# A two-layer hybrid backbone on one core: w_out, the first quarter and the last quarter of the MLP issued in two parts of the tokens

## The chip, the cores and the metric

The kernel runs on one core of one Trainium2 chip. The metric is the device time of one execution in microseconds (us). A profile of one execution comes with it. The engines are TensorE (PE, with its weight loads as PEld), VectorE (DVE), ScalarE (ACT), GpSimd (POOL) and SyncE (SP), which only issues transfers here.

## The reference, cut to what matters

There are 512 latent tokens and 256 context tokens of 1024 channels, and two layers. In layer 0 all 768 tokens are carried through; in layer 1 only the 512 latent ones are (the context is still projected where keys and values need it). A layer is a mixer and an MLP, each with a norm ahead of it and a norm behind it:

```python
hl = modulate(xl, norm_mix_pre[l], mod_l[0], mod_l[1])
oc, ol = token_mixer(hc, hl, cos, sin, w_in[l], rw, cv, at, w_branch[l], w_out[l], ctx_out)
xl = xl + mod_l[2] * rms_norm(ol, norm_mix_post[l])
hl = modulate(xl, norm_mlp_pre[l], mod_l[3], mod_l[4])
xl = xl + mod_l[5] * rms_norm(sq_relu_mlp(hl, w_ff1[l], w_ff2[l]), norm_mlp_post[l])
```

The mixer ends with `jnp.sum(gates * proj, axis=-2) @ w_out`, the MLP is `jnp.square(jax.nn.relu(h @ w1)) @ w2` with 4096 hidden channels. `rms_norm` needs the mean square over all 1024 channels of a token, so it can't begin for a token before the last block of output channels of that token is there. All is float32.

## The kernel before, in words

**Layout.** Activations lie with channels on the partitions and tokens along the free axis: a tensor of 1024 channels is 8 tiles (KT) of 128 x 768. Tokens 0 to 255 are the context, 256 to 767 the latents; `T` is 768 (TOK) in layer 0 and 512 (SEQ) in layer 1.

**A product** of a 128-column block of weights with all tokens is `gemm` (L378) or a `job` (L392) that `fill` (L397) issues one k-step at a time. Weights and activations are split into a high and a low fp32r part, and each of the 8 k-steps issues three products (high x high, high x low, low x high) for each piece of tokens. `pieces` (L117) gives two pieces of 384 tokens in layer 0 and one of 512 in layer 1; a piece lies in one bank of PSUM. So a block is 48 matmuls of 384 columns in layer 0 and 24 of 512 in layer 1.

**Weights** come in halves of 512 x 128 (256 KB), two to a block. `weight_half` (L369) loads one into `raw` (SP queue, L372), ACT rounds it to `wh` (L328) and DVE subtracts to make `wl` (L332). `raw` has two buffers (`nraw`), `wh` and `wl` have three each (`nw`, both set at L1081). Each product that is issued loads its own weights, also the one that is issued again for another piece or another part of the tokens.

**The stages around the change.** `merge_phase` (L1237) multiplies the three branches by w_branch into `acc`, halves `acc` (L1318), splits it, and issues w_out (jobs, L1326); `done` (L1322) copies each block back to `acc`, and `ss_slow` (L313) sums the squares (adds on POOL, a product with ones at L311 for the last two blocks). `rstd` (L281) makes the reciprocal root of the row: a row copy on ACT, small matmuls that turn the row into columns (L291), 12 short DVE instructions, and transposes that spread the result over the partitions (L298). `mlp_phase` (L1335) then loads the residual X, scales and adds it (`post_norm`, L352; L359 and L361), sums squares again, and norms (`norm_h`, L334) into `hh` and `hl`. Only then can w_ff1 begin. The MLP runs in four quarters of the hidden channels: 8 blocks of w_ff1 (L1357) and 8 blocks of w_ff2 (L1371), the latter accumulating into `acc`. After the last quarter the same tail follows: `rstd`, `post_norm`, and in layer 0 the next layer's `norm_h` (L1391), in layer 1 transposes and the store (`store_x`, L1407).

Modulation vectors of layer 0 are made by 16 steps (`mod_steps`, L220) spread over branch 1 and w_out; those of layer 1 by 24 steps over the first three quarters of layer 0's MLP.

**Order.** The program is written in one order, and the tile framework orders it again when it compiles: each engine's queue is fixed then, by a cost model and by priority, the priority being the program's order. On the chip each engine runs its queue in order. In layer 1's mixer `weave` (L1047) issues k-steps of the projection between the steps of the scan, by a ratio; `spills` (L1155) hand it the blocks of q, k, v and of the gates.

Of the kernel before, what the change touches and what calls it, by code (L numbers as in the profile page):

```python
# [18 lines left out]
D = 1024  # L19
# [57 lines left out]
class Kern:  # L77
# [255 lines left out]

    def norm_h(s, sp, X, R, T, gs, sh, hh, hl):  # L334

        nc = s.nc
        o = TOK - T
        for k in range(KT):
            t = sp.tile([128, TOK], F32, tag="nt", name="nt", bufs=2)
            for b, t0, t1 in s.pieces(T, CTX):  # L340
                v = 1 if t0 < CTX else 0
                sl = slice(t0, t1)
                nc.vector.scalar_tensor_tensor(out=t[:, sl], in0=X[:, k, sl], scalar=gs[:, k, v:v + 1], in1=R[:, b, :t1 - t0], op0=ALU.mult, op1=ALU.mult)
                if k % 2:
                    nc.scalar.activation(out=t[:, sl], in_=t[:, sl], func=AF.Identity, bias=sh[:, k, v:v + 1])
                else:
                    nc.scalar.activation(out=hh[:, k, sl], in_=t[:, sl], func=AF.Identity, bias=sh[:, k, v:v + 1])  # L347
                    nc.vector.scalar_tensor_tensor(out=hl[:, k, sl], in0=t[:, sl], scalar=sh[:, k, v:v + 1], in1=hh[:, k, sl].bitcast(F32), op0=ALU.add, op1=ALU.subtract)
            if k % 2:
                s.split(hh[:, k, o:], hl[:, k, o:], t[:, o:], True)  # L350

    def post_norm(s, sp, A, X, R, T, gm, each):  # L352

        nc = s.nc
        o = TOK - T
        for k in range(KT):
            for b, t0, t1 in s.pieces(T, CTX):
                v = 1 if t0 < CTX else 0
                nc.vector.scalar_tensor_tensor(out=A[:, k, t0:t1], in0=A[:, k, t0:t1], scalar=gm[:, k, v:v + 1], in1=R[:, b, :t1 - t0], op0=ALU.mult, op1=ALU.mult)  # L359
            eng = nc.gpsimd if k % 2 else nc.vector  # L360
            eng.tensor_tensor(out=X[:, k, o:], in0=X[:, k, o:], in1=A[:, k, o:], op=ALU.add)  # L361
            each(k)
# [29 lines left out]
    def job(s, src, mh, ml, T, done, pre=None):  # L392

        s.halves += [(src, h) for h in range(2)]
        s.jobs += [(k, mh, ml, T, done, pre) for k in range(KT)]

    def fill(s, n=1):  # L397
        nc = s.nc
        for _ in range(min(n, len(s.jobs))):
            k, mh, ml, T, done, pre = s.jobs.pop(0)  # L400
            if k % 4 == 0:
                while s.halves and len(s.ready) < s.nw:
                    s.ready.append(s.weight_half(*s.halves.pop(0)))
                s.cur = s.ready.pop(0)
            if k == 0:
                s.jps = s.mm()
                s.jctx = (pre(),) if pre else ()
            wh, wl = s.cur
            for w, m, f in ((wh, mh, 0), (wh, ml, 1), (wl, mh, 2)):
                a = m(k)  # L410
                for b, t0, t1 in s.pieces(T):
# [651 lines left out]
    def spill(s, l, r, T):  # L1063

        c0, t, f = s.spills[r]
        T = TOK if t else T
        s.in_job(l, c0, T, lambda ps: s.spill_done(r, T, f, ps))

    def spill_done(s, r, T, tanh, ps):
        nc = s.nc  # L1070
        ft = s.stage()
        if tanh:
            nc.scalar.activation(out=s.dv(ft, T), in_=s.pv(ps, T), func=AF.Tanh, scale=0.5)
        else:
            nc.scalar.activation(out=s.dv(ft, T), in_=s.pv(ps, T), func=AF.Copy)
        nc.scalar.dma_start(s.z[128 * r:128 * r + 128, TOK - T:], ft[:, TOK - T:])


    def run(s):
# [13 lines left out]
        s.z = s.dp.tile([128 * len(s.spills), TOK], F32, name="z")  # L1093
        s.kp = lambda d: d.rearrange("(k p) t -> p k t", p=128)
# [15 lines left out]
        for l in range(DEPTH):  # L1110
# [5 lines left out]
            s.h_open()  # L1116
            s.mlp_phase(l, PP, T, acc, actx)
# [9 lines left out]
    def rwkv_phase(s, l, P, T):  # L1127
# [3 lines left out]
        with ExitStack() as rc:  # L1131
# [21 lines left out]
            todo = list(range(20)) + list(range(28, 36)) + list(range(20, 28))  # L1153

            def spills(n):  # L1155
                for r in todo[:n]:
                    s.spill(l, r, T)
# [79 lines left out]
    def merge_phase(s, l, PP, T, acc):  # L1237
# [4 lines left out]
        with ExitStack() as mc:  # L1242
# [67 lines left out]
            drive(ln, 3)  # L1310
            s.fill(len(s.jobs))
            branch(1, *operand(lambda k: cvx[k]))
            for j in range(KT):
                s.fill(8)
                if steps:
                    steps.pop(0)()
            for k in range(KT):
                nc.vector.tensor_scalar(out=acc[:, k, o:], in0=acc[:, k, o:], scalar1=0.5, scalar2=None, op0=ALU.mult)  # L1318
            hs, ls = operand(lambda k: acc[:, k])
            s.ss = s.ps2()  # L1320

            def done(j, ps):  # L1322
                nc.scalar.activation(out=s.dv(acc[:, j], T), in_=s.pv(ps, T), func=AF.Copy)
                s.ss_slow(lp, s.ss, acc[:, j], j, T)
            for j in range(KT):
                s.job(i['w_out'][l, :, 128 * j:128 * j + 128], lambda k: hs[k], lambda k: ls[k], T, lambda ps, j=j: done(j, ps))  # L1326
            for j in range(KT):
                s.fill(8)
                if steps:
                    steps.pop(0)()  # L1330
            if l == 0:
                s.mod_post(P)
            s.R = s.rstd(lp, s.ss, T, 1.0 / D, 0, CTX)

    def mlp_phase(s, l, PP, T, acc, actx):  # L1335
# [5 lines left out]
        if not last:  # L1341
            PP.append(s.load_params(l + 1))
        X = actx.enter_context(tc.tile_pool(name="x", bufs=1)).tile([128, KT, TOK], F32, name="X")
        for k in range(KT):
            nc.sync.dma_start(X[:, k, o:], s.xT_d[128 * k:128 * k + 128, o:])
        with tc.tile_pool(name="n1", bufs=1) as sp:
            ss = s.ps2()
            s.post_norm(sp, acc, X, s.R, T, P['gm'][0], lambda k: s.ss_add(sp, ss, X[:, k], k, T))
            R = s.rstd(sp, ss, T, 1.0 / D, 0, CTX)
            s.norm_h(sp, X, R, T, P['gs'][1], P['sh'][1], s.hh, s.hl)  # L1350
        with tc.tile_pool(name="mlp", bufs=1) as sp:
            steps = [f for g in range(3) for f in s.mod_steps(l + 1, PP[l + 1], sp, g, 2)] if not last else []
            for q in range(4):
                fhs, fls = [], []
                for j in range(KT):
                    c = q * D + 128 * j
                    ps = s.gemm(i['w_ff1'][l, :, c:c + 128], lambda k: s.hh[:, k], lambda k: s.hl[:, k], T)  # L1357
                    f = sp.tile([128, TOK], F32, tag="f", name="f", bufs=2)
                    nc.scalar.activation(out=s.dv(f, T), in_=s.pv(ps, T), func=AF.Relu)
                    nc.vector.tensor_tensor(out=f[:, o:], in0=f[:, o:], in1=f[:, o:], op=ALU.mult)  # L1360
                    fh = sp.tile([128, TOK], F32R, tag="fh", name="fh", bufs=8)
                    fl = sp.tile([128, TOK], F32R, tag="fl", name="fl", bufs=8)
                    s.split(fh[:, o:], fl[:, o:], f[:, o:])
                    fhs.append(fh)
                    fls.append(fl)
                    if steps:
                        steps.pop(0)()
                if q == 3:
                    ss = s.ps2()
                for j in range(KT):  # L1370
                    ps = s.gemm(i['w_ff2'][l, q * D:(q + 1) * D, 128 * j:128 * j + 128], lambda k: fhs[k], lambda k: fls[k], T)  # L1371
                    if q == 0:
                        nc.scalar.activation(out=s.dv(acc[:, j], T), in_=s.pv(ps, T), func=AF.Copy)
                    else:
                        nc.vector.tensor_tensor(out=s.dv(acc[:, j], T), in0=s.dv(acc[:, j], T), in1=s.pv(ps, T), op=ALU.add)
                    if q == 3:
                        s.ss_slow(sp, ss, acc[:, j], j, T)
            if not last:
                s.mod_pre(PP[l + 1])
                s.mod_post(PP[l + 1])  # L1380
            s.R = s.rstd(sp, ss, T, 1.0 / D, 0, CTX, tag="sq")
        with tc.tile_pool(name="n2", bufs=1) as sp:
            if last:
                s.post_norm(sp, acc, X, s.R, T, P['gm'][1], lambda k: None)
                s.store_x(sp, X)
            else:
# [60 lines left out]
```

## Time and profile before

| | |
|---|---|
| median of 3 runs | 4390.17 us (4380.69 to 4404.21) |
| the profiled execution | 4402.83 us, span of the profile 4401.0 us |
| busy | PE 95%, PEld 77%, DVE 62%, ACT 41%, POOL 7% of the span |
| granted TensorE clock, mean | 0.959 |
| largest shares of the chain that ended last | PE 81%, DVE 8%, ACT 4% |

The profile's times are microseconds from the span's start. A window row gives a stretch and its length; then the busy time of PE, PEld, DVE, ACT and POOL in this order, each with its number of instructions; then the clock that was granted to TensorE as a share of 2.4 GHz, the DMA load as a share, and GB/s. A timeline row gives start, length, engine, line, operation, what is written and read, the shape, and how many instructions it merges; in brackets the idle time before it and what ended it. A mean busy share hides stages: the stretches between the products have to be read one by one.

### The profile page before, as it was taken

Reading aid. Unit: us, or ns where it says so; the run is one execution under the profiler, and the core shown is the slowest. Engines: PE = TensorE matmul, PEld = TensorE weight load, DVE = VectorE, ACT = ScalarE, POOL = GpSimd, SP = SyncE. Lnnn points to the kernel's source line nnn. Section 1 sums busy time; section 2 is a strip of 40 time slices with the busy share of each in tenths; the row PEclk is TensorE's granted clock in tenths of the full one; section 3 lists DMA queues with packets and bytes.
Section 4 is the critical chain, followed back from the end, with each engine's and each line's share of the span. In section 5 each row is a group of like instructions: output and inputs, shape, how many; then the busy total and the mean of one; then the engine's idle time right before and its main releaser. Section 6 shows DMA issues by size and latency. Waiting matters only on the chain.

```text
span 4401.0 us, 76934 instructions
## 1 busy us (share of the span) xinstructions
PE 4180.3 (95%) x31232; PEld 3410.6 (77%) x31232; DVE 2707.6 (62%) x5214; ACT 1819.4 (41%) x3562; POOL 289.9 (7%) x349
## 2 busy tenths in 40 slices
PE   6999999999998989899999899999999989898998
PEld 4888888888886669689999677877777765575886
DVE  3778888878865564332233578888878755454344
ACT  3444444444434442332223345555444534433332
POOL 0000000000001022100000100000000001121001
PEclk9999999999999999899999889999999979998998
DMA  4212111111134235343322221121221232142332
GB/s 167 64 43 65 54 60 55 56 50 60 59 101 157 74 103 162 124 146 121 105 87 64 69 64 54 53 64 55 60 63 52 64 121 79 58 144 60 96 96 79
DMA packets 438346, 364.05 MB, mean 83 GB/s; under 512 B 19022, under 2 KB 386792, under 8 KB 431848
## 3 DMA queue, kind: packets, MB, share of 16 engines
q1 hardware_dynamic: 417256, 279.43, 21.1%
q10 hardware_dynamic: 20736, 79.70, 5.0%
q8 instruction: 247, 4.05, 0.4%
q14 instruction: 107, 0.88, 0.1%
HBM read 299.29 MB, written 53.48 MB: 80 GB/s over the span
## 4 chain that ended last, share of the span: by engine, by line
PE 81%; DVE 8%; ACT 4%; issue 2%; POOL 2%; DMA 2%; SPq 0%; ACTq 0%; POOLq 0%; DVEq 0%
PE mm L412 32%; PE mm L389 20%; PE g L807 4%; PE g L633 2%; PE g L931 2%; PE g L920 2%; PE sp L952 2%; PE g L1032 2%; PE sp L956 1%; PE S L612 1%; PE yp L970 1%; PE g L842 1%; PE yp L968 1%; PE g L816 1%; PE g L234 1%
## 5 line engine op out<-in xcount | busy, mean ns | idle before, releaser
L328 ACT ACTIVATE wh<-raw 128x512 fp32r<-128x512 f32 x700 | 441.9, 631 | 1283.4 <-PE mm L412 590.6
L332 DVE TENSOR_TENSOR wl<-raw,wh 128x512 fp32r<-128x512 f32 x700 | 501.6, 718 | 710.7 <-ACT wh L328 699.1
L412 PE MATMUL mm<-hh,wh 128*128 128x384 f32 (+1 forms) x2072 | 654.2, 373 | 10.2 <-ACT hh L347 4.0
L412 PE MATMUL mm<-hl,wh 128*128 128x384 f32 (+1 forms) x2072 | 640.5, 368 | 7.5 <-POOL hl L330 7.5
L412 PE MATMUL mm<-hh,wl 128*128 128x384 f32 (+1 forms) x2072 | 639.3, 368 | 0.0
L471 DVE SCALAR_TENSOR_TENSOR cv<-u,dw,cv 128x783 f32<-128x783 f32 (+1 forms) x480 | 425.7, 887 | 2.7
L412 PEld LDWEIGHTS mm<-hh,wh 128*128 128x128 f32 x2072 | 379.5, 192 | 54.9 <-issue 6.4
L412 PEld LDWEIGHTS mm<-hl,wh 128*128 128x128 f32 x2072 | 383.7, 192 | 47.7 <-POOL hl L330 10.8
L412 PEld LDWEIGHTS mm<-hh,wl 128*128 128x128 f32 x2072 | 385.7, 193 | 36.7 <-issue 7.2
L412 PE MATMUL mm<-oh,wh 128*128 128x384 f32 (+1 forms) x768 | 253.1, 384 | 9.6 <-DVE acc L1273 6.0
L412 PE MATMUL mm<-ol,wh 128*128 128x384 f32 (+1 forms) x768 | 240.3, 365 | 10.0 <-POOL ol L330 10.0
L389 PE MATMUL mm<-hh,wh 128*128 128x384 f32 (+1 forms) x768 | 239.1, 366 | 6.4 <-ACT hh L347 3.6
L389 PE MATMUL mm<-hl,wh 128*128 128x384 f32 (+1 forms) x768 | 238.0, 364 | 5.5 <-POOL hl L330 5.0
L412 PE MATMUL mm<-oh,wl 128*128 128x384 f32 (+1 forms) x768 | 239.3, 365 | 0.0
L389 PE MATMUL mm<-hh,wl 128*128 128x384 f32 (+1 forms) x768 | 235.7, 362 | 0.0
L389 PE MATMUL mm<-fh,wh 128*128 128x384 f32 (+1 forms) x768 | 229.9, 353 | 0.0
L389 PE MATMUL mm<-fh,wl 128*128 128x384 f32 (+1 forms) x768 | 229.8, 353 | 0.0
L389 PE MATMUL mm<-fl,wh 128*128 128x384 f32 (+1 forms) x768 | 229.5, 352 | 0.0
L807 PEld LDWEIGHTS g<-KR,BK 64*128 64x128 f32 x1536 | 156.6, 206 | 36.8 <-issue 32.4
L412 PEld LDWEIGHTS mm<-oh,wh 128*128 128x128 f32 x768 | 139.9, 190 | 51.3 <-ACT wh L328 13.6
L807 PE MATMUL g<-KR,BK 64*128 64x128 f32 (+1 forms) x1536 | 176.4, 307 | 1.8 <-DVE KR L800 1.6
L958 ACT ACTIVATE S<-sp,lam 128x64 f32<-128x64 f32 x352 | 92.1, 310 | 191.6 <-PE sp L956 182.0
(293 smaller groups left out, 7215.0 us busy)
## 6 DMA issues: line engine op xcount, KB each, us to landing
raw<-in_w_in_dram SPq DMA_DIRECT2D x316, 256.0 KB
raw<-in_w_ff_dram SPq DMA_DIRECT2D x256, 256.0 KB
wmod<-in_w_mod_dram ACTq DMA_DIRECT2D x48, 1024.0 KB
raw<-in_w_branch_dram SPq DMA_DIRECT2D x96, 256.0 KB
z<-f ACTq DMA_DIRECT2D x40, 384.0 KB
gt<-z SPq DMA_DIRECT2D x24, 384.0 KB
raw<-in_w_out_dram SPq DMA_DIRECT2D x32, 256.0 KB
z<-f ACTq DMA_DIRECT2D x32, 256.0 KB
```

The source lines that it names most:

```text
L328: s.last_hi = nc.scalar.activation(out=hi, in_=src, func=AF.Copy)
L332: nc.vector.tensor_tensor(out=lo, in0=src, in1=hi.bitcast(F32), op=ALU.subtract)
L389: nc.tensor.matmul(ps[:, b, :t1 - t0], lhsT=w[:, k % 4, :], rhs=a[:, t0:t1], start=k == 0 and f == 0, stop=k == KT - 1 and f == 2)
L412: s.last_mm = nc.tensor.matmul(s.jps[:, b, :t1 - t0], lhsT=w[:, k % 4, :], rhs=a[:, t0:t1], start=k == 0 and f == 0, stop=k == KT - 1 and ...
L471: s.tap_pin(nc.vector.scalar_tensor_tensor(out=hold['c'], in0=u[:, k:k + L], scalar=w(k), in1=hold['c'], op0=ALU.mult, op1=ALU.add))
L633: nc.tensor.matmul(op[:, :nq], lhsT=V[:, kk, kv * 128:kv * 128 + 128], rhs=PT[:, kk, :nq], start=kk == 0, stop=kk == nk // 128 - 1)
L807: nc.tensor.matmul(gp[h][:, q, 0:n, :], lhsT=BK[ROWS[h], 4 * g + q].rearrange("p a b -> p (a b)"), rhs=KR[ROWS[h], 0:n, 4 * g + q, :], sta ...
L920: nc.tensor.matmul(wu[ROWS[h], q - q0], lhsT=TT[ROWS[h], q, :], rhs=KM[ROWS[h], q].rearrange("p a b -> p (a b)"), start=True, stop=True)
L931: nc.tensor.matmul(ap[ROWS[h], q - q0, 0:n, :], lhsT=W[ROWS[h], q, :], rhs=GB[ROWS[h], h, q, 0:n, :], start=True, stop=True)
L952: nc.tensor.matmul(sp[ROWS[h], d], lhsT=GB[d][:, h, q[d], 0, :], rhs=UV[d][:, h * 12 + q[d], :], start=d == 0, stop=d == 1 and k == 0)
L958: nc.scalar.activation(out=Sn[:, d], in_=sp[:, d], func=AF.Copy, scale=Q['lam', d][:, q[d]:q[d] + 1])
L1032: s.nc.tensor.matmul(o, lhsT=Q['lw'][ROWS[d], i, :], rhs=s.low[ROWS[d], i, t0:t1], start=True, stop=True)
```

## The change

w_out, the first quarter's w_ff1 blocks and the last quarter's w_ff2 blocks are issued twice, once for each of two parts of the tokens. Layer 0: w_out and w_ff1 by tokens 0 to 255, then 256 to 767; w_ff2 by 256 to 511, then 0 to 255 together with 512 to 767 (two pieces). Layer 1: 256 to 511, then 512 to 767, everywhere. The new `residual` is a generator that makes the root, the residual add and the next norm of one part; `weave` runs it with ratio 0.6 while the next part's products are queued as jobs, and `fill` issues the rest. `merge_phase` ends with branch 1; its w_out, and all of `mlp_phase`, become `tail_phase`. The number of `raw`, `wh` and `wl` buffers is not touched. The modulation steps of layer 0 now run in branches 2 and 1. All X adds are on DVE. Eight gate blocks of layer 1's projection (`early`) are issued for tokens 256 to 511 beside the last residual of layer 0, and for 512 to 767 in layer 1's mixer.

```diff
+        s.early = list(range(28, 36))
...
+            if lat:
+                rest_of = {r: [(0, 512, TOK)] for r in s.early}
...
-                    s.spill(l, r, T)
+                    s.spill(l, r, rest_of.get(r, T))
...
+    def rstd_p(s, sp, ss, pcs):
...
+    def residual(s, sp, A, X, ss, pcs, gm, nxt=None):
+        nc = s.nc
+        R = s.rstd_p(sp, ss, pcs)
+        yield 2.0
+        s2 = s.g([128, 512]) if nxt else None
+        for k in range(KT):
+            for t0, t1, r in R:
                 v = 1 if t0 < CTX else 0
+                nc.vector.scalar_tensor_tensor(out=A[:, k, t0:t1], in0=A[:, k, t0:t1], scalar=gm[:, k, v:v + 1], in1=r, op0=ALU.mult, op1=ALU.mult)
+            for t0, t1 in s.spans(pcs):
+                nc.vector.tensor_tensor(out=X[:, k, t0:t1], in0=X[:, k, t0:t1], in1=A[:, k, t0:t1], op=ALU.add)
+            if nxt:
+                sq, n = s.squares(sp, X[:, k], pcs)
+                nc.tensor.matmul(s2[0:1, :n], lhsT=s.ones, rhs=sq, start=k == 0, stop=k == KT - 1)
+            yield 0.5
+        if nxt:
+            R = s.rstd_p(sp, s2, pcs)
+            yield 2.0
+            for k in range(KT):
+                s.norm_k(sp, X, R, k, nxt[0], nxt[1], s.hh, s.hl)
+                yield 0.5
...
+        full = s.pieces(T)
+        if T == TOK:
+            parts, ends = ([(0, 0, CTX)], [(0, CTX, TOK)]), ([(0, CTX, 512)], [(0, 0, CTX), (1, 512, TOK)])
+        else:
+            parts = ends = ([(0, CTX, 512)], [(0, 512, TOK)])
...
+            out_jobs(parts[0], h[0])
+            flush()
+            out_jobs(parts[1], h[1])
+            s.weave(0.6, s.residual(sp, acc, X, h[0]['ss'], parts[0], P['gm'][0], nxt(P, 1)))
+            flush()
+            f0 = []
+            ff1_jobs(0, parts[0], f0)
+            s.weave(0.6, s.residual(sp, acc, X, h[1]['ss'], parts[1], P['gm'][0], nxt(P, 1)))
+            flush()
...
+            ff1_jobs(0, parts[1], f0, each)
+            ff2_jobs(0, full, f0)
+            flush()
+            for q in range(1, 4):
+                fs = []
+                ff1_jobs(q, full, fs, each)
+                if q < 3:
+                    ff2_jobs(q, full, fs)
+                flush()
...
+            ff2_jobs(3, ends[0], fs, h[0])
+            flush()
+            ff2_jobs(3, ends[1], fs, h[1])
+            n = None if last else nxt(N, 0)
+            s.weave(0.6, s.residual(sp, acc, X, h[0]['ss'], ends[0], P['gm'][1], n))
             if last:
+                s.store_x(sp, X, range(2))
+            flush()
+            if not last:
+                for r in s.early:
+                    s.spill(l + 1, r, ends[0])
+            s.weave(0.6, s.residual(sp, acc, X, h[1]['ss'], ends[1], P['gm'][1], n))
+            if last:
+                s.store_x(sp, X, range(2, 4))
             else:
                 nc.sync.dma_start(s.kp(s.xT_d), X)
+            flush()
```

## Rows read from the trace of the kernel before

**Rows 1.** The page: busy time, share of the span and instructions by engine.

```profile
PE 4180.3 (95%) x31232; PEld 3410.6 (77%) x31232; DVE 2707.6 (62%) x5214; ACT 1819.4 (41%) x3562; POOL 289.9 (7%) x349
```

**Rows 2.** Windows, layer 0: w_out, gap, w_ff1; last w_ff2, gap, layer 1's first products.

```profile
1749.00:1829.00 80.00, 78.50 (x460) 68.05 (x456) 18.08 (x23) 22.54 (x33) 18.39 (x12) 1.00 0.45 150
1829.00:1864.00 35.00, 21.64 (x83) 8.82 (x80) 21.00 (x62) 11.86 (x18) 7.25 (x4) 0.77 0.28 98
1864.00:1952.00 88.00, 82.07 (x440) 71.83 (x440) 37.70 (x49) 30.75 (x48) 7.77 (x6) 0.92 0.46 153
...
2375.00:2444.00 69.00, 67.83 (x388) 66.38 (x387) 19.04 (x25) 17.55 (x25) 11.02 (x6) 1.00 0.21 62
2444.00:2479.00 35.00, 21.69 (x79) 8.40 (x77) 20.77 (x51) 11.44 (x17) 7.25 (x4) 0.81 0.26 98
2479.00:2500.00 21.00, 16.46 (x56) 13.07 (x56) 15.00 (x21) 11.35 (x19) 6.86 (x4) 0.66 0.05 13
```

**Rows 3.** The same view, layer 1: w_out, gap, w_ff1 of the first quarter; last w_ff2, tail.

```profile
3934.00:3978.00 44.00, 42.10 (x175) 32.20 (x174) 11.21 (x16) 17.83 (x30) 8.99 (x7) 1.00 0.43 131
3978.00:4007.00 29.00, 16.52 (x44) 5.72 (x43) 14.17 (x40) 9.06 (x15) 6.60 (x4) 0.68 0.06 18
4007.00:4061.00 54.00, 51.67 (x194) 38.90 (x194) 26.04 (x39) 24.50 (x41) 5.10 (x4) 0.89 0.24 71
...
4326.00:4372.00 46.00, 45.13 (x196) 36.04 (x194) 15.26 (x23) 14.40 (x23) 7.70 (x6) 1.00 0.26 75
4372.00:4401.00 29.00, 12.37 (x47) 7.87 (x46) 13.11 (x29) 3.60 (x6) 6.60 (x4) 0.59 0.18 73
```

**Rows 4.** Chain of waits: a modulation step, a run of 384-column, one of 512-column products.

```profile
1759.02 0.99 PE g L234 x8
...
2241.56 191.97 PE mm L389 x1100
...
4016.80 347.69 PE mm L389 x1496
```

**Rows 5.** Weight supply: timeline of SP, ACT and DVE around 3868 us.

```profile
3867.65 4.71 SPq L372 DMA_DIRECT2D raw<-in_w_branch_dram  x3
...
3870.61 0.63 ACT L328 ACTIVATE wh<-raw 128x512 fp32r<-128x512 f32 x1 [2.18 <-DMA raw<-in_w_branch_dram]
3871.27 0.69 DVE L332 TENSOR_TENSOR wl<-raw,wh 128x512 fp32r<-128x512 f32 x1 [0.19 <-ACT wh L328]
```

**Rows 6.** Timeline (DVE, ACT): norm at 256 columns, root, residual at 512, tail.

```profile
2478.42 0.47 DVE L343 SCALAR_TENSOR_TENSOR nt<-X,mc,mm 128x256 f32<-128x256 f32 x1
...
3983.49 0.16 DVE L293 TENSOR_SCALAR rs<-g 128x4 f32<-128x4 f32 x1 [4.13 <-PE g L291]
...
3985.67 0.17 DVE L279 SCALAR_TENSOR_TENSOR rs<-rq 128x4 f32<-128x4 f32 x1
...
3988.37 0.68 DVE L361 TENSOR_TENSOR X<-X,acc 128x512 f32<-128x512 f32 x1
...
4379.95 1.41 DVE L359 SCALAR_TENSOR_TENSOR acc<-acc,mc,mm 128x512 f32<-128x512 f32 x2 [1.21 <-PE mm L298]
...
4388.35 0.60 ACT L1415 ACTIVATE ot<-g 128x512 f32<-128x512 f32 x1 [2.13 <-PE g L1414]
```

**Rows 7.** Timeline, SP: a load of `load_params` (L163) and a later w_out load (L372).

```profile
1754.63 0.30 SPq L163 DMA_DIRECT2D ra<-in_norm_mix_pre_dram  x1
...
1758.58 0.39 SPq L372 DMA_DIRECT2D raw<-in_w_out_dram  x1
```

**Rows 8.** Windows: layer 1's mixer, its attention; timeline (PE): products at a low clock.

```profile
2600.00:3560.00 960.00, 944.79 (x9423) 746.87 (x9421) 788.21 (x1669) 488.16 (x1061) 28.05 (x84) 0.96 0.21 62
3610.00:3810.00 200.00, 168.60 (x614) 98.67 (x613) 99.78 (x190) 85.14 (x174) 12.33 (x9) 0.95 0.27 87
...
2485.62 0.84 PE L412 MATMUL mm<-hh,wh 128*128 128x384 f32 x2
...
2486.26 0.84 PE L412 MATMUL mm<-hl,wh 128*128 128x384 f32 x2
```

More of the change, by code (lines that the diff above doesn't have):

```diff
@@ new lines, in rstd_p @@
+    def rstd_p(s, sp, ss, pcs):
+        nc = s.nc
+        n = sum(t1 - t0 for b, t0, t1 in pcs)
+        row = sp.tile([128, TOK], F32, tag="sq", name="row", bufs=2)[0:1]
+        nc.scalar.activation(out=row[:, :n], in_=ss[0:1, :n], func=AF.Copy, scale=1.0 / D)
+        cps = s.g([128, 8])
+        m = n // 128
+        for t in range(m):
+            nc.tensor.matmul(cps[:, t:t + 1], lhsT=row[0:1, t * 128:(t + 1) * 128], rhs=s.ones[0:1, 0:1], start=True, stop=True)
+        rs = sp.tile([128, 8], F32, tag="rs", name="rs", bufs=2)
+        nc.vector.tensor_scalar(out=rs[:, :m], in0=cps[:, :m], scalar1=EPS, scalar2=None, op0=ALU.add)
+        s.rsqrt(rs[:, :m], s.rq[:, 0, :m], s.rq[:, 1, :m])
+        R = s.ps2()[:, 0]
+        for t in range(m):
+            nc.tensor.transpose(out=R[:, t * 128:t * 128 + 128], in_=rs[:, t:t + 1].to_broadcast([128, 128]), identity=s.ident)
+        out, o = [], 0
+        for b, t0, t1 in pcs:
+            out.append((t0, t1, R[:, o:o + t1 - t0]))
+            o += t1 - t0
+        return out
@@ L394, in job @@
         s.halves += [(src, h) for h in range(2)]
-        s.jobs += [(k, mh, ml, T, done, pre) for k in range(KT)]
+        s.jobs += [(k, mh, ml, T if isinstance(T, list) else s.pieces(T), done, pre) for k in range(KT)]
     def fill(s, n=1):
@@ L1309, in merge_phase @@
             branch(2, *operand(load(s.oat)))
-            drive(ln, 3)
-            s.fill(len(s.jobs))
+            for _ in range(4):
+                for _ in ln:
+                    s.fill(3)
+                    break
+            while s.jobs:
+                for _ in range(2):
+                    next(ln, None)
+                s.fill(8)
+                if steps:
+                    steps.pop(0)()
+            for _ in ln:
+                pass
             branch(1, *operand(lambda k: cvx[k]))
@@ L1314, in merge_phase, with tail_phase @@
                 s.fill(8)
[L1315 to L1330, printed above, removed]
+                for _ in range(2 if len(steps) > KT - j else 1):
+                    if steps:
+                        steps.pop(0)()
             if l == 0:
                 s.mod_post(P)
-            s.R = s.rstd(lp, s.ss, T, 1.0 / D, 0, CTX)
-    def mlp_phase(s, l, PP, T, acc, actx):
+    def tail_phase(s, l, PP, T, acc):
         nc, tc, i, P = s.nc, s.tc, s.i, PP[l]
@@ L1340, in mlp_phase @@
         s.lo_pool = False
[L1341 to L1350, printed above, removed]
@@ new lines, in ff2_jobs, with done @@
+            def ff2_jobs(q, pcs, fs, hold=None):
+                def done(j, ps):
+                    for t, p in s.views(ps, pcs, acc[:, j]):
+                        if q == 0:
+                            nc.scalar.activation(out=t, in_=p, func=AF.Copy)
+                        else:
+                            nc.vector.tensor_tensor(out=t, in0=p, in1=t, op=ALU.add)
+                    if hold is not None:
+                        s.ss_tile(sp, hold, acc[:, j], j, pcs)
+                for j in range(KT):
+                    s.job(i['w_ff2'][l, q * D:(q + 1) * D, 128 * j:128 * j + 128], lambda k: fs[k][0], lambda k: fs[k][1], pcs, lambda ps, j=j: done(j, ps))
```

172 lines of the change are left out of this document (102 added, 70 removed).

## The prediction

> **What bounds the kernel now.** I read the page first: PE is busy for 4180 of 4401 us, DVE for 2708 [rows 1]. So a saving must come out of the stretches in which PE has nothing to issue. The windows around w_out and the MLP's ends show these. In layer 0, 35 us lie between the last product of w_out and the first full run of w_ff1, with PE busy for 21.6 us of them in small products at clock 0.77; then w_ff1's first quarter takes 88 us at clock 0.92. Another 35 us lie behind the last w_ff2, and 21 us of slow start follow [rows 2]. In layer 1 the gap is 29 us, the first quarter takes 54 us, and the tail is 29 us [rows 3]. These gaps are what the change wants to cover.
>
> The chain gives a product's price at full speed: 191.97/1100 = 0.1745 us for 384 columns, 347.69/1496 = 0.2324 us for 512 [rows 4]. No product of 256 columns is in it. Carried on along the same line it is 0.1745 − 0.0579 = 0.117; I take 0.12, and 0.1745 is the upper end (the lower is 0.117, since the line's fixed part does not go away).
>
> What I look for next is how fast weights can come, because every product issued for another part loads its weights again. A half is issued at 3867.65; its rounding starts at 3870.61, 2.96 us later, and takes 0.63; the low part starts at 3871.27 and takes 0.69. Only then is its `raw` buffer free: the third of the three issues ends 4.71 us after the first begins. With 0.39 us off for one issue [rows 7], **two buffers give two halves, one block, in 4.32 us at best** [rows 5]. Today this costs nothing, since a block of 24 x 0.2324 = 5.6 us, or 48 x 0.1745 = 8.4 us, takes longer. A 256-token block is 24 x 0.12 = 2.9 us of PE. It will wait: I take 4.5 us, between 4.32 and an upper end of 4.9 where DVE has other work, so 36 us for 8 blocks, not 23.
>
> **Layer 0, w_out to w_ff1.** Before: 80 + 35 + 88 = 203 us [rows 2]. After: w_out for 256 tokens, 36 (supply). w_out for 512 tokens, 8 x 24 x 0.2324 = 44.6; the first residual (256 tokens) lies beside it, and a block of 5.6 us leaves DVE over 4 us besides its two low parts. w_ff1 for 256 tokens runs beside the residual of 512 tokens, on DVE: 16 low parts of 0.69 = 11 [rows 5]; for f, 16 instructions of half of 0.69 = 5.6; scaling and adding, 8 x (0.70 + 0.68) = 11; two roots of 2.35 (3983.49 to the end of 3985.67); the norm, 8 scalings of 0.70 and 4 low parts of 0.69 = 8.4 [rows 5, 6]: 41 in all, I take 43. w_ff1 for 512 tokens, 44.6 plus 8 modulation steps of 0.99 [rows 4], 52.6. The 8 steps that left w_out cost the branches 8. Sum 184, **−19 us**.
>
> **Layer 0, end.** Before: 69 + 35 + 21, less 9.8 for 56 products done in the 21 (56 x 0.1745), 115 [rows 2, 4]. After: 36 for the first 256 tokens (supply). For the other 512 in two pieces of 256, 8 x 48 x 0.12 = 46 (67 at the upper end). The eight early gate blocks beside the last residual: 36 by supply, 35 on DVE (the 41 above without f); as the low parts stand in one queue with a residual that waits for its two roots, I add 8: 44. Sum 126, **+11 us**. In return layer 1's mixer does those blocks for 256 tokens only, 8 x 24 x 0.1124 = 21.6 us less of PE. PE is busy for 945 of 960 us there, so much of it should be had, but DVE is busy for 788 of them [rows 8] and gets no fewer low parts: between 0 and −21.6 I take **−15**, nearer the full PE.
>
> **Layer 1, w_out to w_ff1.** Before: 44 + 29 + 54 = 127 [rows 3]. After: four passes of 256 tokens at 36, 144: **+17 us**. PE's share of these is 92 us; the gap is covered, but the cover is longer than what it covers.
>
> **Layer 1, end.** Before: 46 + 29 = 75 [rows 3]. After: 36 + 36, then a tail of 256 tokens: 8.0 to the root's end as now (4372 to 4379.95), 8 x (0.47 + 0.35) = 6.6 for scale and add, half of the 12.7 us from the first store copy to the end, 6: 92.6, **+18 us** [rows 3, 6].
>
> **The rest.** Three of layer 1's passes have a residual beside them; at a cycle of 4.7 instead of 4.5 they cost 3 x 8 x 0.2, **+5**. X's loads (3 MB in layer 0, 2 in layer 1) stand ahead of w_out's weights on SP's queue. At the 150 GB/s and load of 0.45 of [rows 2], 333 GB/s, they are 9 and 6 us if nothing covers them; I take 0, since the tile framework moves loads and the attention before them leaves the DMA at 0.27 [rows 8]; the 15 stay for the range. POOL loses its X adds: off the path, 0, and no gain by itself. The spills' stores become 16 of half the size on ACT's queue, which is busy for 41% [rows 1]: 0, at most 8 further issues of 0.39 us as SP's [rows 7], 3. What waits behind a wait: on DVE, a scaling that waits for the root's transposes holds up the low part behind it, and so SP's next issue; that is what the 43, the 44 and the 4.7 contain.
>
> **Sum.** −19 + 11 − 15 + 17 + 18 + 5 = **+16 or 17 us**, by the unrounded terms 16.4. It is made against an execution of 4402.8 us, 12.7 above the median of 4390.2; I put the difference on the median: 4406.6, **4407**. By the bounds: a cycle of 4.32 or 4.9 on the 64 blocks of the eight supply-bound passes, −12 or +26; the mixer, −7 or +15; the two-piece pass, +21 at most; X's loads, +15 at most. All upper ends won't meet; the case's own range is 4380 to 4450.
>
> A rule that bears on the 2.96 us: the trace has issue to rounding only, with whatever queueing is in it [rows 5]. The Trainium skill, page "DMA: Bandwidth & Descriptors", section "Anatomy of one DMA — SWDGE (gpsimd) path", fits a transfer's time as some 2.0 us plus its bytes at 436 GB/s. That fit is for GpSimd's path and not for SP's, which issues here; by it 256 KB would be an estimated 2.6 us, the cycle about 4.0, and the sum some 35 us lower, near 4372. The row is of this very transfer, so the row decides.
>
> **Rivals.**
> *A, the weights keep up.* If the queue ran deeper than the row shows (the 2.96 us would be queueing, not latency), a pass is 23 us by PE. Eight passes gain 8 x 13 = 104, and the crowding of 5 goes; DVE gives some 8 of this back in layer 1. That is 101 below my sum, −84: 4306. For it: PE is the bound everywhere today [rows 1]. Against: in [rows 5] nothing queues ahead of the three issues, and the third still waits for the low part of the first.
>
> *B, the residual isn't covered (the slower side).* `weave` spreads only 0.6 x 12 = 7 of 64 k-steps over a residual; the rest stand behind it in the program. If the queues keep that order, the low parts of the other blocks come behind the whole residual on DVE, and PE stops after the 7. Two residuals of 512 tokens at 29 [rows 3], four of 256 with a norm at 29 − 10 = 19 (half of the 20 us of column work), one without at 9: 143; less 7 x 21 x 0.12 = 18 done meanwhile, and less 20 of DVE crowding that I have in the sum: 105 more, 4512. It decides if fewer than about half of a pass's low parts get ahead of the residual. Against it: the order is made anew by the tile framework, and a parameter load issued in the program after w_out stands ahead of a w_out weight load [rows 7].
>
> *C, the clock falls in the passes.* A pass with PE busy 2.9 of 4.5 us may be granted 1.2 GHz. Then two 384-column products started 0.64 us apart, 0.32 each [rows 8]; 256 columns would be 0.213, a block 5.1 us, longer than the supply, +0.6 on each of 64 blocks: 39 more, 4446. For it: clocks of 0.59 to 0.81 in the gaps [rows 2, 3]. Against it: in the attention PE is busy for 84% of 200 us and the clock stays 0.95 [rows 8], though a pass at 64% lies lower. The Trainium skill, page "Perfetto Trace Analysis", section "Matmul Optimizations", says that engine power scales with use and that matmuls should be issued back to back; that speaks for C and against any change that trades a few long gaps for many short ones.
>
> *D, nothing happens:* the order before already covers the gaps. The windows exclude it: the gaps are there [rows 2, 3].
>
> **How the numbers follow.** The main case has 0.71, A 0.08, B 0.06, C 0.15, D 0. A difference of 0.5%, 22 us, is about what a measurement can tell here: faster is below 4368, slower above 4412. The main case's own 0.71 is 0.09 faster (a short cycle and the whole mixer gain), 0.35 within, 0.27 slower. With A: faster 0.17; same 0.35; slower 0.27 + B + C = 0.48. The range leaves out A, B and the ends of the rest, 0.2 together: 4368 to 4466, C inside. The likeliest case's own range is 4380 to 4450.
>
> **What would show it.** Right: in 256-token passes weight issues come about 2.2 us apart, PE's idle time ends with `wh` or `wl`, eight blocks take 35 to 39 us, the three long gaps are gone, the tail is near 20 us, and layer 1's two stretches are longer than before while layer 0's first is shorter. Wrong: passes of 23 to 28 us (A); gaps of 20 us or more inside the passes, with `wl` behind residual instructions (B); clocks below 0.8 in passes whose PE idles little (C). A mixer of layer 1 as long as before would take the −15 away, and X's loads just ahead of w_out's weights, with SP late, would show the +15.

## The result, and the profile after

The changed kernel takes **4501.34 us** (median of 4 runs, 4492.17 to 4502.68) against 4390.36 before: ratio 1.0251, interval 1.0224 to 1.0277. It is 111 us slower; 4407 was forecast, with a range to 4466. The profiled execution's span is 4490.4 us, 89.4 above the 4401.0 of before. (The profiled run of before lay 13 us above its median, that of after 9 below its own, at mean granted clocks of 0.959 and 0.965; the stretches below account for the 89.4.)

The page of the changed kernel, its line of busy times, as in [rows 1]:

```profile
PE 4215.6 (94%) x32216; PEld 3442.0 (77%) x32216; DVE 2818.3 (63%) x5578; ACT 1910.6 (43%) x3841; POOL 269.2 (6%) x377
```

PE is busy for only 35 us more, and the span is 89 longer. So at least 54 us are new idle time, in spite of the gaps that were to go. The windows of the changed kernel, pass by pass (columns as in [rows 2]; the first four are layer 0's w_out in two passes and w_ff1 in two, the next three its end, the last four layer 1's w_out, w_ff1, last w_ff2 and tail):

```profile
1749.00:1794.00 45.00, 32.90 (x197) 28.76 (x198) 19.25 (x20) 20.18 (x37) 14.56 (x13) 0.89 0.60 200
1794.00:1847.00 53.00, 51.96 (x223) 37.38 (x222) 27.16 (x69) 27.14 (x55) 11.25 (x11) 1.00 0.29 85
1847.00:1919.00 72.00, 55.62 (x331) 31.01 (x330) 38.23 (x91) 29.30 (x56) 5.68 (x6) 0.88 0.61 201
1919.00:1967.00 48.00, 48.00 (x197) 37.29 (x196) 21.86 (x35) 19.15 (x34) 0.00 (x0) 0.96 0.39 119
2385.00:2474.00 89.00, 82.37 (x615) 73.31 (x615) 48.92 (x110) 38.04 (x79) 16.74 (x18) 1.00 0.33 95
2474.00:2530.00 56.00, 39.90 (x231) 28.40 (x229) 36.37 (x96) 27.52 (x67) 8.40 (x17) 0.91 0.44 140
2530.00:2549.00 19.00, 17.91 (x101) 17.41 (x102) 6.94 (x12) 6.58 (x12) 0.00 (x0) 1.00 0.38 107
3967.00:4046.00 79.00, 64.56 (x420) 53.35 (x419) 42.80 (x86) 41.42 (x90) 19.38 (x22) 0.96 0.41 124
4046.00:4131.00 85.00, 62.74 (x415) 52.15 (x413) 48.22 (x114) 40.71 (x86) 2.90 (x4) 0.92 0.34 98
4397.00:4471.00 74.00, 61.78 (x413) 53.02 (x411) 37.12 (x77) 26.82 (x50) 9.79 (x14) 0.95 0.39 117
4471.00:4490.00 19.00, 6.39 (x25) 3.81 (x24) 9.57 (x31) 1.98 (x4) 0.00 (x0) 0.65 0.14 55
```

By the first and last product of each stretch, the 89 us come from here:

| stretch | before, us | after, us | difference | forecast |
|---|---|---|---|---|
| all before layer 0's w_out | 1749.0 | 1749.5 | +0.5 | +8, in the branches |
| layer 0, w_out to the end of w_ff1's first quarter | 203.3 | 217.2 | +13.9 | −27 |
| layer 0, the MLP's middle | 422.8 | 418.0 | −4.8 | 0 |
| layer 0, last w_ff2 to layer 1's 96th product | 132.6 | 163.8 | +31.2 | +11 |
| layer 1, mixer, to w_out | 1426.3 | 1418.2 | −8.1 | −15 |
| layer 1, w_out to the end of w_ff1's first quarter | 126.9 | 164.4 | +37.5 | +22 |
| layer 1, middle | 265.4 | 265.8 | +0.4 | 0 |
| layer 1, last w_ff2 and tail | 74.7 | 93.5 | +18.8 | +18 |

The first row hides a cost. The eight modulation steps that moved to the branches did cost about what was forecast: the three branches take 379.7 us from their first product to their last, against 371.0 before. They begin 11 us earlier (1366.2 against 1377.2), behind layer 0's mixer, whose work the change leaves as it was; why that was shorter in this execution is not shown. In the middle, 3.5 of the 4.8 us are modulation products that now run in the stop described below.

**Two patterns** stand in these passes. The first is the forecast one. Timeline of the changed kernel, SP, then ACT and DVE, in a pass with no residual beside it (layer 1, first part of the last w_ff2):

```profile
4402.30 16.53 SPq L445 DMA_DIRECT2D raw<-in_w_ff_dram  x9
...
4404.96 0.63 ACT L344 ACTIVATE wh<-raw 128x512 fp32r<-128x512 f32 x1 [0.94 <-DMA raw<-in_w_ff_dram]
...
4405.62 0.69 DVE L348 TENSOR_TENSOR wl<-raw,wh 128x512 fp32r<-128x512 f32 x1 [1.46 <-ACT wh L344]
```

Nine issues in 16.53 us are eight steps of 2.02, so 4.03 us for a block of two halves; ACT waits for the load, DVE for ACT, and PE's own work for the block is 2.9.

The second pattern is a long stop. The same view in layer 0's first w_ff1 pass (PE, then ACT), and below it layer 1's second w_out pass (ACT, DVE, PE):

```profile
1855.89 0.28 PE L486 MATMUL mm<-hh,wl 128*128 128x256 f32 x1
...
1858.34 7.03 PE L428 MATMUL g<-sq,ones 128*1 128x512 f32 x12 [2.17 <-ACT sq L397]
...
1886.07 1.93 PE L250 MATMUL g<-wmod,sc 128*32 128x512 f32 x8 [0.57 <-DMA wmod<-in_w_mod_dram]
1887.93 0.58 PE L486 MATMUL mm<-hh,wh 128*128 128x256 f32 x1
...
1886.02 0.72 ACT L365 ACTIVATE nt<-nt,mod 128x512 f32<-128x512 f32 x1 [1.50 <-POOL hl L346]
1886.64 0.36 ACT L1446 ACTIVATE f<-mm 128x256 f32<-128x256 f32 x1
...
1890.12 0.63 ACT L344 ACTIVATE wh<-raw 128x512 fp32r<-128x512 f32 x1 [0.83 <-PE mm L486]
...
4007.54 0.63 ACT L344 ACTIVATE wh<-raw 128x512 fp32r<-128x512 f32 x1 [0.19 <-DMA raw<-in_w_out_dram]
...
4014.43 0.77 DVE L425 TENSOR_TENSOR X<-X,acc 128x256 f32<-128x256 f32 x2
4015.10 1.30 DVE L348 TENSOR_TENSOR wl<-raw,wh 128x512 fp32r<-128x512 f32 x2
...
4016.38 0.39 PE L486 MATMUL mm<-fh,wl 128*128 128x256 f32 x1
```

PE issues no product of w_ff1 from 1855.89 to 1887.93, 32 us, after exactly two blocks (48 products). What it runs meanwhile are sums of squares, a root and six modulation steps. At 1890.12 the rounding of the next weights waits for PE, not PE for it. The output f of the first block, done long before, is written only at 1886.64, right behind nearly all of the norm's nt. In layer 1 a half's low part comes at 4015.10, though its high part had been ready since 4008.2: sixteen scalings and adds of the residual stand ahead of it on DVE, and PE waits 5.9 us.

### The profile page after: what moved, and what is told of

The parts are those of the page before. It is cut to its first block, busy times and chain, and to the rows that moved or that the text cites. A ratio compares the mean times of both kernels' runs of the same rounds, so it can differ in the third digit from the quotient of the medians.

```text
span 4490.4 us, 80065 instructions
## 1 busy us (share of the span) xinstructions
PE 4215.6 (94%) x32216; PEld 3442.0 (77%) x32216; DVE 2818.3 (63%) x5578; ACT 1910.6 (43%) x3841; POOL 269.2 (6%) x377
## 5 line engine op out<-in xcount | busy, mean ns | idle before, releaser
L486 PE MATMUL mm<-hh,wh 128*128 128x384 f32 (+2 forms) x2968 | 925.2, 362 | 45.7 <-ACT wh L344 28.3
L486 PE MATMUL mm<-hh,wl 128*128 128x384 f32 (+2 forms) x2968 | 907.1, 358 | 8.0 <-DVE wl L348 7.9
L486 PE MATMUL mm<-hl,wh 128*128 128x384 f32 (+2 forms) x2968 | 904.4, 356 | 1.6 <-POOL hl L346 1.6
L486 PEld LDWEIGHTS mm<-hl,wh 128*128 128x128 f32 x2968 | 552.5, 192 | 47.8 <-issue 7.6
L486 PE MATMUL mm<-fh,wh 128*128 128x256 f32 (+2 forms) x1152 | 339.6, 331 | 26.1 <-ACT wh L344 22.1
L486 PE MATMUL mm<-fh,wl 128*128 128x256 f32 (+2 forms) x1152 | 340.9, 332 | 9.7 <-DVE wl L348 9.6
L486 PE MATMUL mm<-fl,wh 128*128 128x256 f32 (+2 forms) x1152 | 337.4, 329 | 3.7 <-POOL fl L346 2.8
L486 PEld LDWEIGHTS mm<-fh,wh 128*128 128x128 f32 x1152 | 213.8, 192 | 48.6 <-ACT wh L344 30.5
L486 PEld LDWEIGHTS mm<-fh,wl 128*128 128x128 f32 x1152 | 214.5, 193 | 30.6 <-DVE wl L348 17.7
L486 PEld LDWEIGHTS mm<-fl,wh 128*128 128x128 f32 x1152 | 214.6, 193 | 19.6 <-issue 4.4
```

## The experiments

Differences are between medians; the changed kernel is 4501.34.

**1. A third raw buffer.**

```diff
-        s.nraw, s.nw, s.lo_pool, s.turn = 2, 3, False, 0
+        s.nraw, s.nw, s.lo_pool, s.turn = 3, 3, False, 0
```

> The changed kernel with three raw buffers instead of two (room is made by cutting the tail's rows of squares to 512 columns). Supply theory: each 256-token pass is paced by two raw buffers at one block per 4.1 us; with three the cycle is 2.7 us, under PE's 2.9, and passes without a residual (last quarter first part in both layers, w_out's first part, layer 1's second w_ff1 pass) fall from 34 to 44 us to 24 to 30; in all 70 to 110 us faster than the changed kernel, near 4390 to 4430. Queue theory (the holes behind the residual's instructions cost the most): the passes keep their holes of 5 to 32 us, and the time falls by under 30 us.

4448.79 us, 52.6 less. Windows (layer 0's first w_ff1 pass; layer 1's two w_out passes; its two w_ff1 passes; its last two), and SP's row within the last, one fence each:

```profile
1845.00:1912.00 67.00, 55.16 (x321) 31.63 (x320) 37.91 (x90) 28.98 (x54) 5.86 (x6) 0.85 0.60 194
3968.00:4036.00 68.00, 60.93 (x423) 52.96 (x424) 43.61 (x87) 40.97 (x93) 20.14 (x22) 0.95 0.50 151
4036.00:4107.00 71.00, 55.10 (x412) 49.71 (x411) 45.63 (x111) 37.97 (x85) 2.90 (x4) 0.90 0.39 112
4373.00:4435.00 62.00, 54.45 (x410) 50.27 (x408) 36.17 (x78) 26.42 (x50) 10.48 (x14) 0.97 0.45 133
```

```profile
4375.48 9.84 SPq L445 DMA_DIRECT2D raw<-in_w_ff_dram  x7
```

Layer 1's three pairs of passes lose 11, 14 and 12 us; a block's weights now come every 3.15 us (six steps in 9.84 less one issue of 0.39) instead of 4.03. The 32 us stop stays (72 us of window became 67). So supply paces the passes, and it is about half of the loss, not all: the gain lies between the two theories' figures.

**2. The residual spread over the whole pass.**

```diff
-            s.weave(0.6, s.residual(...))
+            s.weave(5.3, s.residual(...))
```

> The changed kernel with the weave ratio 5.3 in place of 0.6 in the four residuals, so that the 64 k-steps of a pass are issued evenly between the residual's steps. Queue theory, in its form that the program's order sets the queues: the holes of 5 to 32 us beside the residuals are gone or halved, 30 to 60 us faster than the changed kernel. If the framework's own reordering sets them: within 10 us of the changed kernel. Supply theory alone: also within 10 us, since the number of raw buffers is the same.

4462.33 us, 39 less. Windows (layer 0's first w_ff1 pass; layer 1's w_out; its w_ff1):

```profile
1849.00:1893.00 44.00, 38.98 (x256) 27.60 (x258) 33.71 (x83) 22.72 (x44) 1.26 (x1) 1.00 0.40 124
3947.00:4022.00 75.00, 65.17 (x419) 53.52 (x419) 43.56 (x86) 39.80 (x89) 19.85 (x22) 0.95 0.43 129
4022.00:4097.00 75.00, 63.15 (x414) 51.82 (x414) 47.85 (x114) 39.12 (x86) 3.56 (x4) 0.98 0.39 113
```

The pass of 72 us takes 44, layer 1's 79 and 85 take 75 each, and no stop over 3 us is left in layer 1 (in layer 0 one of 8.5 us is left beside the early blocks, in place of 5.9 and 9.5). The program's order does reach the chip, though the framework orders anew.

**3. Low parts on POOL beside a residual.** `lo_pool` set from w_out's second part to w_ff1's first, and in the last quarter's second part.

> The changed kernel with the weights' low parts on POOL in the passes that lie beside a residual. Queue theory, in its form that low parts wait behind the residual on DVE: the holes of 5 to 11 us go (six of them, 45 us), the passes are a little longer for POOL's slower subtraction, 15 to 35 us faster in all; the 32 us hole stays unless it too is a low part's. Supply theory alone: slower by 5 to 20 us, since a half's cycle gets longer on POOL.

4519.76 us, 18 more. Groups by form, layer 1's w_out and w_ff1 (POOL, DVE), of this kernel:

```profile
L346 POOL TENSOR_TENSOR wl<-raw,wh 128x512 fp32r<-128x512 f32 x32 | 41.6, 1304 | 36.2 <-ACT wh L344 31.4 <-PE mm L486 4.7
...
L1450 DVE TENSOR_TENSOR f<-f 128x256 f32<-128x256 f32 x15 | 9.6, 642 | 15.4 <-ACT f L1446 15.4
```

and of the changed kernel in the same stretch:

```profile
L1450 DVE TENSOR_TENSOR f<-f 128x256 f32<-128x256 f32 x15 | 6.3, 423 | 4.9 <-ACT f L1446 4.8
```

A low part takes 1.30 us on POOL against 0.69 to 0.72 on DVE, which lengthens the supply's cycle, and DVE's own f got slower beside it. Layer 0's long stop stayed (its pass took 80 us instead of 69), so low parts on DVE are not what makes that one. The shorter stops went both ways. In layer 1, the longest in w_out is now 3.7 us instead of 5.9, and at the end 2.4 instead of 5.2, but the two in w_ff1 (7.1 and 11.0) became one of 18.5; beside the early blocks 5.9 and 9.5 became one of 5.7.

**4. Modulation steps later.** `each` is not passed to w_ff1's second part of layer 0.

> The changed kernel with layer 1's modulation steps begun in the second quarter of layer 0's MLP, not in the second part of the first. If these steps, waiting for their loads at the head of PE's queue, make the hole of 32 us in layer 0's first w_ff1 pass: the hole falls to some 17 us, 10 to 20 us faster. If the residual alone holds it: the hole stays at 28 to 32 us and the time within 8 us.

4501.18 us: no change. The pass took 73.3 us by its products, and its stop was as long as before. But the edit did not move what it aimed at. The last row of PE ahead of the next w_ff1 product (at 1890.05):

```profile
1888.19 1.94 PE L250 MATMUL g<-wmod,sc 128*32 128x512 f32 x8 [0.88 <-DMA wmod<-in_w_mod_dram]
```

The framework put the same six steps (48 products, 9.5 us of PE, 7.2 us of waits for their loads) into the stop again. So this run says nothing on them. In the changed kernel f is there at 1887.0 and the last step ends at 1888.0, and ACT's norm waited 2.3 us for one of the steps: what part of the 32 us is theirs stays open.

**5. Three raw buffers and the even order together.**

> The changed kernel with both of the edits that helped alone: three raw buffers (alone 52 us faster than the changed kernel) and the weave ratio 5.3 (alone 39 us faster). If weight supply and the order of the queues are two separate causes, their gains add up: 91 us faster than the changed kernel, near 4410. If the holes only hide slack of the supply, or the other way round, the second gives less than half of its own gain: 4425 to 4445.

4411.17 us, 90.2 less; the two gains alone add up to 91.6. Windows, layer 1's w_out, w_ff1 and last w_ff2:

```profile
3953.00:4017.00 64.00, 58.84 (x420) 51.17 (x420) 42.98 (x86) 39.34 (x89) 19.24 (x21) 0.97 0.52 158
4017.00:4077.00 60.00, 54.92 (x412) 49.27 (x411) 45.80 (x114) 37.54 (x86) 4.32 (x5) 0.97 0.46 133
4343.00:4401.00 58.00, 53.66 (x412) 50.52 (x411) 36.46 (x78) 26.11 (x50) 11.61 (x14) 0.97 0.49 144
```

Supply and order are two separate causes, and together 90 of the 111 us.

**6. Layer 1 not split.** `parts` and `ends` are not used in layer 1: all 512 tokens at once, each residual beside nothing.

> The changed kernel with layer 1 not split (w_out, first quarter and last quarter by 512 tokens, residuals beside nothing, as before); layer 0 as changed. By the stretches of the two profiles layer 1's split costs 37 us behind w_out and 19 us at the end, so 56 us faster than the changed kernel, near 4445, and the rest, some 45 us over the kernel before, is layer 0's. If a part of the loss only moves (a slower start after the gaps that come back), 30 to 45 us faster.

4436.80 us, 64.5 less (ratio 1.0125 to before). Windows of w_out, gap and w_ff1 in layer 1, to be held against [rows 3]:

```profile
3969.00:4017.00 48.00, 47.00 (x194) 36.77 (x194) 16.88 (x19) 21.13 (x38) 14.69 (x11) 0.96 0.41 127
4017.00:4044.00 27.00, 14.18 (x43) 4.26 (x42) 16.18 (x43) 8.59 (x15) 0.00 (x0) 0.77 0.06 18
4044.00:4094.00 50.00, 48.26 (x192) 37.39 (x193) 26.21 (x39) 24.10 (x40) 5.23 (x4) 0.95 0.26 74
```

The gap of 27 us is back, and it is cheaper than its cover. Layer 1's split costs about 60 us (56 by the table, 64.5 by the medians), layer 0's the other 46 (4436.80 against 4390.36).

**7. The residual's squares summed on POOL**, with two products by ones at its end instead of eight (`ss_tile`'s way).

> The changed kernel with the squares of the new residual summed on POOL, with two products by ones instead of eight for each residual. If the eight products, each waiting for its squares at the head of PE's queue, hold the weight products behind them: the 31 us hole in layer 0's first w_ff1 pass falls under 20, the holes beside layer 1's residuals by half, and some 15 us of PE work go; 15 to 35 us faster. If the low parts behind the residual on DVE hold them: the holes stay within 4 us and the time falls by 0 to 10 us.

4532.50 us, 31 more. One window, layer 0's first w_ff1 pass:

```profile
1856.00:1933.00 77.00, 50.54 (x316) 30.82 (x314) 40.82 (x90) 28.16 (x53) 14.73 (x13) 0.80 0.58 187
```

Neither theory allowed for a loss. The six adds took 1.41 us each on POOL, so the residual's chain got longer, and the pass with it (72 us to 77, its stop 32 to 39). That speaks for the residual's end as what holds the products, not its small products.

**8. No early gate blocks.** `s.early = []`.

> The changed kernel without the eight early gate blocks: layer 1's mixer does them for all 512 tokens, and the last residual of layer 0 lies beside nothing. Supply theory: the early pass of 56 us becomes a gap of some 30 us, the mixer gets 7 to 15 us longer: 10 to 20 us faster. If the early blocks are worth their cover: 5 to 20 us slower.

4479.30 us, 22 less. Windows, layer 0's last w_ff2 and what follows it:

```profile
2387.00:2478.00 91.00, 83.08 (x610) 74.32 (x609) 48.91 (x108) 37.67 (x78) 16.82 (x18) 0.98 0.31 91
2478.00:2505.00 27.00, 15.51 (x49) 4.85 (x47) 17.04 (x60) 8.30 (x21) 0.00 (x0) 0.81 0.30 109
```

A gap of 27 us stands where the early pass took 56. The mixer, from its first long run of 512-column products to the end of its projections, took 1060.9 us (2556.2 to 3617.1), against 1069.0 in the changed kernel (2577.6 to 3646.6). Windows of these two stretches, the changed kernel's first:

```profile
2577.00:3647.00 1070.00, 1035.38 (x10065) 820.48 (x10064) 841.21 (x1802) 525.24 (x1143) 35.57 (x90) 0.93 0.20 60
2556.00:3617.00 1061.00, 1036.29 (x10067) 815.36 (x10066) 843.22 (x1808) 527.53 (x1146) 31.07 (x90) 0.95 0.21 61
```

The granted clock was 0.95 here and 0.93 there, so the shorter mixer does not show that the gate blocks cost nothing whole. The kernel before, which also does them whole, took 1076.1 us at 0.93. The early pass gives way to a gap 29 us shorter, and the time falls by 22: some 7 us come back elsewhere, as the supply theory had it.

**9. A buffer of its own for f.**

```diff
-                    f = sp.tile([128, TOK], F32, tag="nt", name="f", bufs=2)
+                    f = sp.tile([128, TOK], F32, tag="f", name="f", bufs=2)
```

> The changed kernel with a buffer of its own for w_ff1's output f, which shares the two buffers nt with the residual's norm (room: rows of squares and nt cut to 512 columns, the parameter loads moved ahead of the tail's pool). In the trace the first f is written at 1886.64, just behind the last nt, and PE stopped after exactly two blocks, as many as the two product buffers in PSUM hold. Buffer theory (f stands behind the norm for its buffer, so PSUM stays full): the 31 us hole in layer 0 falls under 10 and the 11 us one in layer 1 goes; 25 to 45 us faster than the changed kernel. Queue theory (the low parts behind the residual on DVE hold the products): the hole stays over 20 and the time within 12 us.

4478.76 us, 22.6 less, a little under the buffer theory's 25 and outside the queue theory's 12. The first pass of w_ff1 in layer 0, and layer 1's two (windows); then ACT's first f:

```profile
1855.00:1905.00 50.00, 42.06 (x266) 28.09 (x264) 39.08 (x81) 28.02 (x54) 5.19 (x4) 0.97 0.40 124
4040.00:4117.00 77.00, 63.35 (x418) 51.27 (x417) 47.62 (x114) 40.44 (x87) 3.08 (x4) 1.00 0.38 111
```

```profile
1860.65 0.36 ACT L1453 ACTIVATE f<-mm 128x256 f32<-128x256 f32 x1
```

f is written 5.9 us after the pass begins instead of 39.6. The 32 us without a product became stops of 9.5 and 5.9, and layer 1's of 11 us is gone. The second of these stops ends with modulation steps (PE; the next w_ff1 product starts at 1894.32):

```profile
1892.45 1.94 PE L250 MATMUL g<-wmod,sc 128*32 128x512 f32 x8 [2.74 <-DMA wmod<-in_w_mod_dram]
```

The 5.9 us stop in layer 1's w_out stayed (6.1): there no f is written, and the low parts wait on DVE, as the changed kernel's rows above show.

**10 and 11. Combined.** Three raw buffers, ratio 5.3, no early blocks, modulation steps from the second quarter on (the framework left five of them in the first, as in 4 it left six); in 11 besides layer 1 not split.

> Three raw buffers and the ratio 5.3 (together 4411), and besides no early gate blocks (alone 22 us faster) and layer 1's modulation steps from the second quarter on (alone 0; but with the even order a wait of 4.0 us for their loads now stands in the 8 us hole behind layer 0's first w_ff1 pass). If all gains add: 4382. If the early pass's loss was mostly its supply, which the third buffer has mended: 4395 to 4405.

> As the combined kernel, with layer 1 not split. In the profile of the kernel with three buffers and the even order layer 1's stretches took 125 and 78 us, against 127 and 75 unsplit in the kernel before: within 8 us of the combined kernel. If layer 1's split still costs its 64 us in part: 10 us or more faster.

4383.34 us, ratio to before 0.9979 (0.9961 to 0.9997), and 4380.22 us, 0.9973 (0.9955 to 0.9991). Windows of the second: layer 0's w_out and first quarter; its end; layer 1's w_out and first quarter:

```profile
1749.00:1936.00 187.00, 173.71 (x886) 130.19 (x887) 108.08 (x210) 92.74 (x176) 31.69 (x26) 0.96 0.46 145
2360.00:2494.00 134.00, 117.20 (x761) 97.01 (x754) 79.98 (x202) 59.56 (x128) 25.05 (x35) 0.92 0.31 96
3909.00:4034.00 125.00, 109.20 (x428) 78.62 (x429) 59.18 (x101) 53.66 (x90) 20.04 (x15) 0.92 0.28 82
```

4383 is near the 4382 of all gains added. By their medians both lie 0.2 to 0.3% under the kernel before, but no stretch shows a gain. Layer 0's first stretch takes 187 us against 203, its end 134 against 133, layer 1 125 against 127. Modulation products in the first stretch, before and in experiment 11 (windows of their line alone: PE and PEld, then clock and DMA):

```profile
1749.00:1953.00 204.00, 17.01 (x132) 2.52 (x128) 0.92 0.42 141
1749.00:1936.00 187.00, 5.47 (x40) 0.89 (x40) 0.96 0.46 145
```

So 11.5 of the 16 us are work that lies elsewhere now, most of it in the branches, and these take 382.7 us instead of 371.0. From the branches' first product to the end of w_ff1's first quarter it is 573.5 us against 575.1: even. The lower medians come with a higher granted clock. The kernel before took 4367.6 to 4371.2 us in its three executions at 0.968 to 0.970, and up to 4407.5 in the others, at 0.957 to 0.965. Experiments 10 and 11 took 4371.1 to 4393.0, at 0.965 to 0.972. At an equal clock neither is faster; whether the new order itself raises the clock is not shown. Whether the third buffer alone would help the kernel before was not tried.

**12. X's loads behind w_out's first part.**

> The changed kernel with X's loads issued behind w_out's first part instead of ahead of it. If they hold up the weights on SP's queue: the 9 us between two weight issues at the pass's start fall to 5, layer 0's first pass from 44 to 36 to 40 us, the time 3 to 10 us less. If the supply alone paces the pass: no change, within 4 us.

4489.07 us (4487.16 to 4494.80), 12 less, but the pass it aimed at took 44.0 us against 44.1. SP's rows say why:

```profile
1753.60 2.73 SPq L1473 DMA_DIRECT2D X<-xT_d  x6
1765.35 0.99 SPq L445 DMA_DIRECT2D raw<-in_w_out_dram  x2
```

The framework put six of the eight loads ahead of the weights again. The edit did not do what it set out to do; what X's loads cost stays open, and the 12 us are not explained.

## Why the prediction was wrong, step by step

**The supply term was right.** "It will wait: I take 4.5 us ... so 36 us for 8 blocks, not 23." Layer 1's passes of 8 blocks without a residual took 37 to 42, and experiment 1 moved them by adding a buffer. My "at best" was a little long: clean cycles are 4.0 to 4.2 us, issue to rounding mostly 2.6 to 2.9. The Trainium skill's fit (page "DMA: Bandwidth & Descriptors", section "Anatomy of one DMA — SWDGE (gpsimd) path"), for another path, gave an estimated 2.6 and a cycle of 4.0; these rows agree with it. Its sum, 4372, would have gone further off, since supply was not the missing part.

**The step that failed** is the overlap: "w_ff1 for 256 tokens runs beside the residual of 512 tokens". I took 43 us for this pass from a sum of DVE's work, as if residual and products ran side by side. It took 69, because two things put the products behind the residual. One is the buffer: f and the norm's nt share two buffers under one tag, which are handed out in the program's order, and the ratio 0.6 issues 7 k-steps beside the residual, so that the whole norm comes ahead of the first f, which needs 8. Then two finished blocks fill PSUM, and PE stops until the norm is through. I named SP's, DVE's and POOL's queues, and no buffer. Experiment 9 shows it: 32 us fell to 9.5 and 5.9. The other is DVE's queue, with low parts behind sixteen residual instructions (layer 1, 5.9 us); the even order takes nearly all of both away, for 39 us in all. The modulation steps in the 32 us stop are a third candidate for a part of it, which experiment 4 did not test.

**Rival B had the rule, not the places.** It said that queues keep the program's order, so that the residual isn't covered, and gave 4512, near the 4501 measured. But it priced seven bare residuals at 105 us over my sum. The stops over 3 us beside residuals measure 32 + 5.9 + 9.5 in layer 0 and 5.9 + 7.1 + 11.0 + 5.2 in layer 1, 77 us in all, and layer 0's first residual was covered as forecast (no stop over 2.2 us in its pass of 53 us). That 4512 lies near 4501 is in part luck: B lacked the losses of w_out's two parts, 17 us, which follow. My evidence against B, a parameter load that the framework had moved ahead, was a load without a wait for a buffer; it says nothing of tiles that take turns in one. The chance of 0.06 was too low.

**Term by term.** Layer 0's first stretch: 43 was 69 (the stop), w_out's second part 44.6 was 53.8: PE is busy for 52.0 us of that window, and its transposes and ones products for the first residual, which I had left out, lie in the 512-column pass, where PE is the bound. W_ff1's second part, 52.6, was 48.2, since six of its modulation steps had run in the stop. W_out's first part, 36, was 44: a stop of 4.5 us stands near its start. There SP issues the next weights at 1769.26, 3.8 us after a buffer came free at 1765.47 (0.03 us is usual), with layer 1's parameter loads in between. X's loads had gone out before (1748.48 to 1752.87), while SP's next weights came at 1760.22, when DVE had finished splitting acc and the first of two low parts; which of these cost what stays open, as experiment 12 moved too little. My range had a term for SP's queue, my sum had 0. Layer 0's end: 36 + 46 was 89, 44 for the early blocks was 56.5 (stops of 5.9 and 9.5). The mixer, −15, was −8; how much of this the early blocks gave is open, since the granted clock differed too (experiment 8). The branches' +8 came as forecast (8.7), hidden by the earlier start. Layer 1's first stretch, +22, was +37: 24 us of stops in it. Layer 1's end, +18: +19.

**The other rivals.** A (weights keep up) is out: two buffers don't keep up. C (1.2 GHz in the passes) is out: 1.2 GHz would be a granted clock of 0.5, and it is 0.92 to 0.96 in layer 1's passes; the lower windows (0.88, 0.89, 0.91 in layer 0) are passes with stops in them. The Trainium skill's advice to issue matmuls back to back (page "Perfetto Trace Analysis", section "Matmul Optimizations") agrees with that, but it explains little of the loss: the clock did not halve in any pass.

## What to carry to other kernels

Splitting a product to cover a stage loads its weights again: put the supply's cycle per block, from issue to the buffer's release, beside the shorter block before anything else. Then list every buffer that the covering work shares with the covered one, and ask in what order the program hands it out; a shared tag with two buffers is a queue as binding as an engine's. Interleave the two pieces of work evenly in the program if the order decides, and compare the cover's own price with the gap (here 27 us, cheaper bare in layer 1). When a stretch gets shorter, look where its work went, and at which granted clock the two executions ran, before you call it a gain.

## What was not expected of the hardware

With the low parts on POOL, DVE got slower on work that had not changed: f times f for 256 columns took 642 ns on average instead of 423, the X add 521 instead of 424. The scalings, which read one of their two tensors from PSUM, did not (472 and 479 ns); why is not tested. POOL needed 1.30 us for a subtraction of 512 columns that takes DVE 0.69 to 0.72. An idle POOL was no free resource beside a busy DVE.
